# One encoder layer on one core: one of four weight sums per seven-product group on another engine

## The chip, the cores and the metric

The kernel runs on one core of one Trainium2 chip. The metric is the device time of one execution in microseconds, as the median of several runs.

## The reference

One layer of an encoder trunk is computed in float32 on 512 tokens of width 2048. What matters here is the second half of the layer, the feed-forward part; the first half (two kinds of sequence mixing, of which only the time is of interest) comes before it.

```python
y = jnp.concatenate([y_attn, y_lru], axis=-1) @ w_out[l]
h = layer_norm(DEEPNORM_ALPHA * h + y, ln1_g[l], ln1_b[l])
f = jnp.square(jax.nn.relu(h @ w_up[l])) @ w_down[l]     # 2048 -> 8192 -> 2048
h = layer_norm(DEEPNORM_ALPHA * h + f, ln2_g[l], ln2_b[l])
```

## The kernel before

Features lie on the partitions, tokens along the free dimension. Every matrix product with float32 accuracy is made of three products in the faster fp32r type: an operand is split into a high half (a copy to fp32r on ScalarE, ACT) and a low half (operand minus high half, on VectorE, DVE), and TensorE (PE) multiplies high by high, high by low and low by high (`product`, lines 831 to 833: eight blocks of 128 rows, 24 matmuls of 128x256 in all).

Most of the feed-forward part is done in groups of seven block products instead of eight (`winograd`, line 838): 30 groups for `w_up` and 27 for `w_down`, 57 in all. A group loads four weight tiles of 128x1024 (`wload`: a11, a21, a22, a12; the DMAs stand on SyncE's queue, SP). From them four sums are made in place on DVE by the helper `tt` (line 836), in this order in the program: T3's sum a11 - a21 into a11, T1's sum a21 + a22 into a21, T2's sum a22 - a11 into a11, and B22's sum a12 - a11 into a12. The seven products B11, T3, T1, X4, B21, B22 and T2 go through PE in that order. Each one's weight is split by `wsplit` (line 799) right before it: line 153 is the copy on ACT that writes `whi`, line 154 the subtraction on DVE that writes `wlo`. There are three buffers for `whi` and three for `wlo` (two in one pool, one in another), so a split for a product can begin only when the product three places earlier is done with its half. The weight tiles themselves have seven buffers (`wraw`, line 813). T1's sum writes the tile that T3's sum reads.

Results of a group stay in four accumulators in PSUM; DVE adds two partial sums (s1, s7) and the group's results, ACT squares them (in the `w_up` part), and a further operand set is written to DRAM (`up_out`).

The operands of the products (oph, opl) stay in SBUF over many groups and are changed four times: once between the two weight matrices and three times within the second. At these places `u_load` (line 872) loads them and splits them on ACT and DVE, and one or two plain products (`classic`, line 720) run in between.

The order of the instructions on each engine's queue is set when the program is built: a planner takes what is ready in its own account of time, by priority; the splits of weights have a priority 100 places ahead of their line. Engines work through their queues in order and wait for each other by semaphores. GpSimd (POOL) does a few small powers for the norms and, at the very end, three normalising instructions (line 190); in the groups it does nothing.

Of the kernel before, what the change touches and what calls it, by code (L numbers as in the profile page):

```python
# [13 lines left out]
ALU = mybir.AluOpType  # L14
# [34 lines left out]
def body(tc, x, pos, vecs, consts, w_in, w_uq, w_kn, w_v, w_rg, w_out, w_up, w_down, out):  # L49
    nc = tc.nc  # L50
    V, A, T, G = nc.vector, nc.scalar, nc.tensor, nc.gpsimd
# [747 lines left out]
    def wsplit(f, n):  # L799
        woff[0] = (32, 0) if n in ("T3", "T1") else FAR  # L800
        with tc.high_priority(offset=PO2):
            w = wsplit_(f)
        woff[0] = FAR
        return w
# [15 lines left out]
    def wload(src):  # L820
        t = wraw(rawn[0])
        rawn[0] += 1
        nc.sync.dma_start(out=t, in_=src)
        return t

    def product(acc, w, n, first):
        wh, wl = w
        sk = dict(skip_group_check=not first)
        for j in range(8):
            ws = slice(j * P, (j + 1) * P)  # L830
            T.matmul(acc, wh[:, ws], oph[n][:, j], start=first and j == 0, stop=False, **sk)  # L831
            T.matmul(acc, wh[:, ws], opl[n][:, j], start=False, stop=False, **sk)  # L832
            T.matmul(acc, wl[:, ws], oph[n][:, j], start=False, stop=j == 7, **sk)  # L833

    def tt(o, x, y, op):
        V.tensor_tensor(out=o, in0=x, in1=y, op=op)  # L836

    def winograd(slabs, evac, hook=lambda n: None):

        a11 = wload(slabs[0])  # L840
        a21 = wload(slabs[2])
        a22 = wload(slabs[3])
        a12 = wload(slabs[1])
        bank = lambda tag, bufs: ps.tile([P, HS], F32, tag=tag, name="st_" + tag, bufs=bufs)
        half = lambda n: ws_p.tile([P, HS], F32, tag=n, name=n, bufs=2)
        a, b, c, d = bank("mm", 3), bank("sc", 2), bank("tr", 3), bank("mm", 3)
        s1, s7 = half("s1"), half("s7")
        product(a, wsplit(a11, "B11"), "B11", True)
        hook("B11")
        A.activation(s1, a, AF.Copy)  # L850
        tt(a11, a11, a21, ALU.subtract)
        product(b, wsplit(a11, "T3"), "T3", True)
        A.activation(s7, b, AF.Copy)  # L853
        tt(a21, a21, a22, ALU.add)
        product(c, wsplit(a21, "T1"), "T1", True)
        tt(s7, s7, c, ALU.add)
        product(b, wsplit(a22, "X4"), "X4", False)
        hook("X4")
        tt(a11, a22, a11, ALU.subtract)
        product(a, wsplit(a12, "B21"), "B21", False)  # L860
        hook("B21")
        evac("c11", a, None)
        tt(a12, a12, a11, ALU.subtract)
        product(c, wsplit(a12, "B22"), "B22", False)
        hook("B22")
        product(d, wsplit(a11, "T2"), "T2", True)
        tt(s1, s1, d, ALU.add)
        evac("c21", s1, b)
        evac("c12", s1, c)
        evac("c22", s1, s7)  # L870
# [13 lines left out]
    for ch in range(NCL, DFF // 256):  # L884
        o = o_tile()

        def evac(which, x, y):
            t = o[:, 2 * int(which[1]) + int(which[2]) - 3, :]
            if y is not None:
                tt(t, x, y, ALU.add)  # L890
                x = t
            A.activation(t, x, AF.Relu)
            A.activation(t, t, AF.Square)
        winograd([w_up[4 * ch + i] for i in range(4)], evac,
                 *([next_ops(0)] if ch == DFF // 256 - 1 else ()))
        up_out(ch, o)
# [46 lines left out]
    for c in range(NCH):  # L943
        if c == 0:
            r_init(0)
        for i in range(KT // 2):
            sl = [w_down[(c * KT + 2 * i) * 2 + q] for q in range(4)]
            if c == NCH - 1 and i == KT // 2 - 1:
                last_pair(sl)
            elif i < NCL2:  # L950
                def evac(n, acc):
                    tt(r[2 * i + n], r[2 * i + n], acc, ALU.add)
                classic(sl, evac, [lambda n=n: u_load(c, n, n) for n in ("T3", "T1", "T2")] if i == 0 else ())
                if i == NCL2 - 1:
                    u_load(c, "T4", "X4")
            else:
                q = rp[i]

                def evac(which, x, y):
                    t = q[:, 2 * int(which[1]) + int(which[2]) - 3, :]  # L960
                    if which == "c11":
                        tt(t, t, x, ALU.add)
                    elif which == "c22":
                        tt(y, y, x, ALU.add)
                        tt(t, t, y, ALU.add)
                    else:
                        tt(t, t, y, ALU.add)
                        tt(t, t, x, ALU.add)
                def prev_stats(n, i=i):
                    if n == "X4" and i == KT // 2 - 2:  # L970
                        u_load(c, "B12", "X4")
                    if n == "B21":
                        for k in (2 * i - 2, 2 * i - 1):
                            to_tokens(r[k], st2, k)
                hook = () if c + 1 < NCH and i < KT // 2 - 1 else \
                    (next_ops(c + 1),) if c + 1 < NCH else (prev_stats,)
                winograd(sl, evac, *hook)
# [69 lines left out]
```

## Time and profile before

| | us |
|---|---|
| median of 3 runs (lowest to highest) | 1984.33 (1983.44 to 1989.12) |
| the profiled execution: its own time | 1982.85 |
| its span, first to last instruction | 1981.1 |
| PE busy in the span | 1931.8 (98%) |
| DVE busy | 1500.4 (76%) |
| ACT busy | 1013.2 (51%) |
| POOL busy | 18.4 (1%) |

The busy time of an engine is the time in which at least one of its instructions runs; matmuls overlap each other, so PE's busy time says that it was fed, not how well. The mean granted clock of TensorE was 0.998 of full speed. The groups of seven products lie between about 740 and 1940 us of the span.

### The profile page before, as it was taken

The numbers are of one execution on the slowest core, as the hardware profiler recorded it, in microseconds if no ns is written. First come the engines' busy times: TensorE is split into PE (matmuls) and PEld (weight loads), VectorE is DVE, ScalarE is ACT, GpSimd is POOL, SyncE is SP. The second block draws the span as 40 slices with busy tenths as digits, with TensorE's granted clock in tenths as the row PEclk, the third lists the DMA queues.
The fourth block names the chain that finished last, engine by engine and source line by source line (L and its number), as shares of the span: only waits on it lengthen the run. The fifth ranks groups of instructions, "written<-read, shape, count | busy, mean of one in ns | idle before, by whom it ended". The sixth has DMA issues, their size and how long they took to land.

```text
span 1981.1 us, 39297 instructions
## 1 busy us (share of the span) xinstructions
PE 1931.8 (98%) x16472; PEld 1899.5 (96%) x16472; DVE 1500.4 (76%) x2147; ACT 1013.2 (51%) x1482; POOL 18.4 (1%) x20
## 2 busy tenths in 40 slices
PE   6999999999999999999999999999999999999997
PEld 6999999888999999999999999999999999999997
DVE  7565655677433598888888888888898888889885
ACT  6556556555322455555555555565464455445453
POOL 1000000000000000000000000000000000000001
PEclk9999999999999999999999999999999999999999
DMA  7222222212233345444544445486364355346232
GB/s 258 80 96 91 88 100 85 65 53 71 96 118 111 122 152 192 170 171 156 184 151 171 171 153 186 152 287 225 127 214 165 111 180 196 116 138 246 101 103 86
DMA packets 113889, 284.19 MB, mean 143 GB/s; under 512 B 10160, under 2 KB 56368, under 8 KB 109616
## 3 DMA queue, kind: packets, MB, share of 16 engines
q1 hardware_dynamic: 113712, 281.68, 41.3%
q8 instruction: 129, 2.11, 0.4%
q14 instruction: 48, 0.39, 0.1%
HBM read 234.19 MB, written 46.14 MB: 142 GB/s over the span
## 4 chain that ended last, share of the span: by engine, by line
PE 87%; DVE 4%; ACT 3%; DMA 2%; issue 2%; POOL 1%; POOLq 0%; SPq 0%; ACTq 0%; DVEq 0%
PE st_mm L831 8%; PE st_mm L832 8%; PE st_mm L833 8%; PE mm L135 7%; PE mm L136 7%; PE mm L134 7%; PE st_tr L833 5%; PE st_sc L831 5%; PE st_sc L833 5%; PE st_tr L831 5%; PE st_tr L832 5%; PE st_sc L832 5%; PE mm L718 1%; PE mm L716 1%; PE mm L717 1%
## 5 line engine op out<-in xcount | busy, mean ns | idle before, releaser
L153 ACT ACTIVATE whi<-raw 128x1024 fp32r<-128x1024 f32 x399 | 423.5, 1063 | 513.2 <-DVE raw L836 251.9
L154 DVE TENSOR_TENSOR wlo<-raw,whi 128x1024 fp32r<-128x1024 f32 x399 | 484.4, 1221 | 128.8 <-ACT whi L153 121.4
L836 DVE TENSOR_TENSOR raw<-raw 128x1024 f32<-128x1024 f32 x228 | 278.2, 1220 | 3.6
L122 DVE TENSOR_TENSOR wlo<-raw,whi 128x1024 fp32r<-128x1024 f32 (+1 forms) x128 | 141.2, 1104 | 166.8 <-PE mm L136 112.1
L121 ACT ACTIVATE whi<-raw 128x1024 fp32r<-128x1024 f32 (+1 forms) x128 | 123.1, 967 | 203.3 <-PE mm L135 159.8
L134 PE MATMUL mm<-hh,whi 128*128 128x256 f32 x704 | 195.4, 278 | 2.7 <-ACT xp L403 1.9
L136 PE MATMUL mm<-hh,wlo 128*128 128x256 f32 x704 | 195.5, 278 | 0.8 <-DVE wlo L122 0.8
L135 PE MATMUL mm<-hl,whi 128*128 128x256 f32 x704 | 196.0, 278 | 0.0
L134 PEld LDWEIGHTS mm<-hh,whi 128*128 128x128 f32 x704 | 132.8, 189 | 3.1 <-ACT xp L403 2.1
L136 PEld LDWEIGHTS mm<-hh,wlo 128*128 128x128 f32 x704 | 132.9, 189 | 1.0 <-DVE wlo L122 1.0
L135 PEld LDWEIGHTS mm<-hl,whi 128*128 128x128 f32 x704 | 132.9, 189 | 0.0
L831 PE MATMUL st_sc<-X4h,whi 128*128 128x256 f32 x456 | 126.6, 278 | 2.2 <-ACT s L853 2.2
L831 PE MATMUL st_tr<-B22h,whi 128*128 128x256 f32 x456 | 126.6, 278 | 1.9 <-ACT whi L153 1.9
L833 PE MATMUL st_sc<-T3h,wlo 128*128 128x256 f32 x456 | 126.5, 277 | 1.0 <-DVE wlo L154 1.0
L831 PE MATMUL st_mm<-B21h,whi 128*128 128x256 f32 x456 | 126.0, 276 | 0.5 <-ACT s L850 0.5
L831 PE MATMUL st_mm<-T2h,whi 128*128 128x256 f32 x456 | 126.0, 276 | 0.4 <-ACT whi L153 0.4
L833 PE MATMUL st_tr<-B22h,wlo 128*128 128x256 f32 x456 | 126.1, 277 | 0.2 <-DVE wlo L154 0.2
L832 PE MATMUL st_sc<-X4l,whi 128*128 128x256 f32 x456 | 126.3, 277 | 0.0
L831 PE MATMUL st_sc<-T3h,whi 128*128 128x256 f32 x456 | 126.1, 277 | 0.0
L833 PE MATMUL st_sc<-X4h,wlo 128*128 128x256 f32 x456 | 126.1, 277 | 0.0
L832 PE MATMUL st_sc<-T3l,whi 128*128 128x256 f32 x456 | 126.1, 277 | 0.0
L833 PE MATMUL st_mm<-B11h,wlo 128*128 128x256 f32 x456 | 126.0, 276 | 0.0
(440 smaller groups left out, 6464.5 us busy)
## 6 DMA issues: line engine op xcount, KB each, us to landing
raw<-in_w_up SPq DMA_DIRECT2D x128, 512.0 KB, 3.4
raw<-in_w_down SPq DMA_DIRECT2D x128, 512.0 KB, 3.5
u_dram<-uo SPq DMA_DIRECT2D x32, 1024.0 KB, 3.8
raw<-in_w_in SPq DMA_DIRECT2D x50, 512.0 KB, 3.2
raw<-in_w_out SPq DMA_DIRECT2D x32, 512.0 KB, 3.2
X4l<-u_dram SPq DMA_DIRECT2D x18, 512.0 KB, 5.3
x<-in_x SPq DMA_DIRECT2D x8, 512.0 KB, 7.0
h_dram<-hf SPq DMA_DIRECT2D x32, 128.0 KB, 2.5
```

Of the source, the lines that this page charges most:

```text
L121: A.activation(hi[:, :w], raw[:, :w], AF.Copy)
L122: V.tensor_tensor(out=lo[:, :w], in0=raw[:, :w], in1=hi[:, :w].bitcast(F32), op=ALU.subtract)
L134: T.matmul(acc[:, c], wh, xh[:, c], start=first and t == 0, stop=False)
L135: T.matmul(acc[:, c], wh, xl[:, c], start=False, stop=False)
L136: T.matmul(acc[:, c], wl, xh[:, c], start=False, stop=last and t == 1)
L153: A.activation(hi, f, AF.Copy)
L154: V.tensor_tensor(out=lo, in0=f, in1=hi.bitcast(F32), op=ALU.subtract)
L716: T.matmul(o, wh[:, ws], oph[b][:, j], start=first and t == 0, stop=False)
L831: T.matmul(acc, wh[:, ws], oph[n][:, j], start=first and j == 0, stop=False, **sk)
L832: T.matmul(acc, wh[:, ws], opl[n][:, j], start=False, stop=False, **sk)
L833: T.matmul(acc, wl[:, ws], oph[n][:, j], start=False, stop=j == 7, **sk)
L836: V.tensor_tensor(out=o, in0=x, in1=y, op=op)
```

## The change

T1's sum goes from DVE to GpSimd: same operands, same place in the program. The two other lines shown are unchanged and stand for the place.

```diff
         tt(a11, a11, a21, ALU.subtract)
         product(b, wsplit(a11, "T3"), "T3", True)
         A.activation(s7, b, AF.Copy)
-        tt(a21, a21, a22, ALU.add)
+        G.tensor_tensor(out=a21, in0=a21, in1=a22, op=ALU.add)
         product(c, wsplit(a21, "T1"), "T1", True)
         tt(s7, s7, c, ALU.add)
```

## Rows read from the trace of the kernel before

**Rows 1.** Stretches: length, busy PE, PEld, DVE, ACT, POOL (instructions); clock, DMA, GB/s.
```profile
1200.00:1219.08 19.08, 19.08 (x171) 19.08 (x170) 16.00 (x20) 10.41 (x17) 0.00 (x0) 1.00 0.46 165
...
1633.68:1652.76 19.08, 18.77 (x165) 18.57 (x164) 19.08 (x22) 10.70 (x11) 0.00 (x0) 1.00 0.93 316
```
**Rows 2.** Waits of PE, 740 to 1940 us: total us, times, longest.
```profile
PE st_sc L831 <- ACT s L853: 2.2, 3, 1.3
...
PE st_sc L833 <- DVE wlo L154: 1.0, 2, 0.5
...
PE st_tr L833 <- DVE wlo L154: 0.2, 1, 0.2
```
**Rows 3.** Instructions of line 836: count, shortest/median/longest ns, first and last start.
```profile
L836 DVE TENSOR_TENSOR raw<-raw x228: 1204/1219/1226, 742.7 to 1923.8; 128x1024 f32<-128x1024 f32 x114
```
**Rows 4.** DVE in order of time, one group: start us, us, instruction, count, idle before.
```profile
1199.73 2.48 DVE L836 TENSOR_TENSOR raw<-raw 128x1024 f32<-128x1024 f32 x2
1202.14 1.23 DVE L154 TENSOR_TENSOR wlo<-raw,whi 128x1024 fp32r<-128x1024 f32 x1
...
1203.62 1.22 DVE L836 TENSOR_TENSOR raw<-raw 128x1024 f32<-128x1024 f32 x1
1204.75 1.22 DVE L154 TENSOR_TENSOR wlo<-raw,whi 128x1024 fp32r<-128x1024 f32 x1
...
1206.88 1.22 DVE L154 TENSOR_TENSOR wlo<-raw,whi 128x1024 fp32r<-128x1024 f32 x1
...
1213.62 2.38 DVE L154 TENSOR_TENSOR wlo<-raw,whi 128x1024 fp32r<-128x1024 f32 x2 [0.85 <-ACT whi L153]
1217.55 1.23 DVE L154 TENSOR_TENSOR wlo<-raw,whi 128x1024 fp32r<-128x1024 f32 x1 [1.54 <-ACT whi L153]
```
**Rows 5.** ACT in order of time, the same group.
```profile
1201.05 1.06 ACT L153 ACTIVATE whi<-raw 128x1024 fp32r<-128x1024 f32 x1 [1.89 <-DVE raw L836]
1202.76 1.07 ACT L153 ACTIVATE whi<-raw 128x1024 fp32r<-128x1024 f32 x1 [0.65 <-PE st_mm L832]
1205.48 1.06 ACT L153 ACTIVATE whi<-raw 128x1024 fp32r<-128x1024 f32 x1 [1.65 <-PE st_mm L832]
```
**Rows 6.** Groups by line from 1960 us (busy, mean ns), and DVE's line 190.
```profile
L190 POOL TENSOR_SCALAR R<-R,mvh,rsh 128x512 f32<-128x512 f32 x3 | 6.7, 2253 | 0.1
L190 DVE TENSOR_SCALAR R<-R,mvh,rsh 128x512 f32<-128x512 f32 x4 | 2.3, 611 | 0.0
L190 DVE TENSOR_SCALAR R<-R,mvh,rsh x25: 535/540/832, 680.1 to 1974.2; 128x512 f32<-128x512 f32 x25
```
**Rows 7.** PE in order of time, where T3 and T1 begin, the same group.
```profile
1205.63 0.28 PE L833 MATMUL st_sc<-T3h,wlo 128*128 128x256 f32 x1
1208.13 0.28 PE L831 MATMUL st_tr<-T1h,whi 128*128 128x256 f32 x1
1208.36 0.28 PE L833 MATMUL st_tr<-T1h,wlo 128*128 128x256 f32 x1
```
**Rows 8.** DVE's sums and PE's T3 products behind two operand changes, by time.
```profile
1651.97 2.48 DVE L836 TENSOR_TENSOR raw<-raw 128x1024 f32<-128x1024 f32 x2
1660.27 0.28 PE L831 MATMUL st_sc<-T3h,whi 128*128 128x256 f32 x1
1809.69 1.22 DVE L836 TENSOR_TENSOR raw<-raw 128x1024 f32<-128x1024 f32 x1
1813.42 1.22 DVE L836 TENSOR_TENSOR raw<-raw 128x1024 f32<-128x1024 f32 x1
1815.97 2.35 DVE L154 TENSOR_TENSOR wlo<-raw,whi 128x1024 fp32r<-128x1024 f32 x2
1816.34 0.28 PE L831 MATMUL st_sc<-T3h,whi 128*128 128x256 f32 x1
```
**Rows 9.** SP's issues in order of time, and DVE's wait for loads, 740 to 1940.
```profile
1206.00 2.46 SPq L823 DMA_DIRECT2D raw<-in_w_up  x2
DVE wlo L154 <- DMA raw<-in_w_up: 3.1, 2, 1.5
```

## The prediction

> **What bounds the kernel now.** I read first the table of stretches. In the part with the seven-product groups (from 740 to 1940 us) one group takes 19.08 us, and PE is busy for 19.08 of them at the full clock (1.00), DVE for 16.00, ACT for 10.41, POOL for nothing [rows 1]. So PE sets the pace there and DVE has 3.08 us of each group left. Then I read the waits of PE over the same 1200 us: seven rows, from 2.2 us down to 0.2 us (2.2 + 1.9 + 1.0 + 0.5 + 0.4 + 0.3 + 0.2), 6.5 us in all, some 0.5% of the stretch [rows 2]. That is the most that any help to DVE or ACT can give back there. Last I read one steady group in order of time on DVE, ACT and PE, to see how long before its use each weight half is ready; this decides whether a slower sum is noticed.
>
> **The change part by part.** It takes from each of 57 groups one sum on DVE and puts it on POOL. The line of the helper has 228 sums of this kind, four to a group, with a median of 1219 ns [rows 3], so DVE loses 57 x 1.22 = 69.5 us of work. PE does not wait for DVE's share of work but for single instructions, so by [rows 2] the removal alone is worth between 0 and 6.5 us; I take 0, since none of these waits stands in the steady groups.
>
> Where the sum stands: at 1199.73 DVE runs two sums, T3's and T1's, 2.48 us together. T3's ends at 1199.73 + 1.22 = 1200.95, T1's at 1202.21 [rows 4]. T1's sum writes a21, which T3's reads, so on POOL it can't begin before 1200.95. The same kind of hand-over from DVE to ACT takes 0.10 us: ACT's copy for T3 starts at 1201.05 [rows 5]. I let POOL start at 1201.05 as well.
>
> What it costs on POOL: the trace has no sum of this size there. The low end is DVE's own 1.22 us. POOL's only large instructions are three with 128x512 elements, two arithmetic steps and one input, 2253 ns each [rows 6]. Scaled by elements to 1024 this gives 4.51 us, the high end; scaled by arithmetic steps (512 x 2 there, 1024 x 1 here) it gives 2.25 us. I take 2.25 us, the value of the nearest row with an equal count of steps, and keep both ends. The Trainium skill's "GPSIMD Engine Reference" (section "Elementwise — side-by-side cycle accounting") gives 4497 ns for this sum with 2048 elements, so an estimate of 2.25 us for 1024 by that page; no run here shows it.
>
> With 2.25 us the sum is ready at 1203.30, 1.09 us later than now. First ACT: its copy for T1 starts at 1202.76, held until then by the weight buffer and not by the sum, and takes 1.07 us [rows 5]. It would start at 1203.40 and end at 1204.47. PE's first T1 product with that half starts at 1208.13 [rows 7]: 3.7 us to spare. ACT's next copy, at 1205.48, waits for PE and is not touched. Then DVE: T1's second half now runs 1204.75 to 1205.97 [rows 4], after ACT's copy in both cases, and PE asks for it at 1208.36 [rows 7]: 2.4 us to spare. Ahead of it DVE's queue has T3's half (1202.14) and T2's sum (1203.62), which don't depend on POOL; behind it stand the group's results and X4's half. So with engines that don't disturb each other nothing is late and DVE is even 1.2 us earlier.
>
> Does POOL hold up DVE? No row has a DVE instruction with two SBUF inputs beside a large one of POOL. The nearest are the four normalising ones of DVE while POOL's three run: 611 ns in the mean against a median of 540 and a longest of 832 [rows 6], so the low end is next to nothing per instruction, and the high end is that DVE stands still while POOL works. The Trainium skill's "SBUF — State Buffer" (section "Who interferes with whom") states the high end as a rule: a DVE instruction with two SBUF inputs and a reading GpSimd instruction exclude each other, and the second waits for the whole of the first. Rows 6 can't confirm it, since those DVE instructions have one input.
>
> At the high end DVE's next two-input instruction, T3's half at 1202.14, starts at 1203.30, 1.16 us late. It ends at 1204.52; PE asks for it at 1205.63 [rows 4, 7], 1.1 us to spare. All that follows on DVE is 1.16 us late too: T1's half ends at 1207.13 against 1208.36 (1.2 us to spare), X4's at 1206.88 + 1.22 + 1.16 = 1209.26 against 1211.09 (one product after T1's use, 1208.36 - 1205.63 = 2.73 us; 1.8 us to spare). The idle gaps of 0.85 and 1.54 us [rows 4] then take up the 1.16 us before the next group. DVE's load would be 16.00 - 1.22 + 2.25 = 17.03 us of 19.08. So in the steady groups the cost is 0 with either end.
>
> The stretches where the operands are changed are tighter: from 1633.68 on DVE is busy for all 19.08 us [rows 1]. But there T3's sum runs at 1651.97 while PE begins T3 only at 1660.27 [rows 8], so 1.1 us is hidden. At the last change T3's sum is at 1809.69 and T1's at 1813.42, before two halves that start at 1815.97 [rows 8]; PE starts T3 at 1816.34, and by the waits it stands 0.5 us for a half in that neighbourhood. There I bound the change by -0.5 (relieved of the sum) and +1.05 (blocked) and take +0.5. With four such changes the bounds are -2 and +4 us.
>
> The DMA queue: a21's buffer comes free with T1's half, at most 1.2 us later. SP issues two loads at 1206.00, just after that half [rows 9]; seven buffers and four loads a group put the next user of the slot 1.75 groups (33 us) on. In the whole first part DVE waits for a weight load for 3.1 us in two cases [rows 9]. No cost.
>
> Sum against the profiled execution of 1982.85 us: 1982.85 + 0 (57 steady places) + 0.5 = 1983.4. The median of the three runs, 1984.33, lies 1.5 us above that execution, so I expect about 1985 in the median.
>
> **The rivals.**
> 1. POOL needs near 4.5 us and DVE is shut out meanwhile (slower). POOL runs 1201.05 to 1205.56; T3's half ends at 1206.78, PE wanted it at 1205.63: 1.15 us late in every group, since each group's chain hangs on PE's own progress and starts with the same lead again. 57 x 1.15 = 66 us, 2049 us. DVE's load of 16.00 - 1.22 + 4.51 = 19.29 us also passes 19.08. It decides from a sum of 3.4 us on (1205.63 - 1.22 - 1201.05 = 3.36). For it: POOL's rows by element. Against it: the count of steps, and that both conditions are needed; with 4.5 us alone T1's copy ends at 1206.7 and its half at 1207.9, still before 1208.36. This is where the rule of the page on SBUF would act; by it and the page on GPSIMD together (2.25 us) the time would stay.
> 2. The order of the queues changes (slower). The queues' order is fixed when the program is built. If T1's copy is put behind X4's because its sum is late, it takes the next free weight buffer, the one whose copy now starts at 1205.48 [rows 5], and ends at 1206.54; its half then ends at 1207.9 at the earliest, 0.5 us ahead of PE. One more two-input instruction of 1.22 us ahead of it makes it 0.7 us late: 57 x 0.7 = 40 us, 2023 us; a part of the groups or a part of the 0.7 us gives less. Against it: the slack is used up only if several things coincide.
> 3. DVE's relief ends PE's waits (faster). At most 6.5 us, 1978 in the median. Against it: these waits hang on single instructions, mostly ACT's, at the changes of operands.
>
> **How the numbers follow.** No change: 0.70, with 1982 to 1989 as its own range; rival 1: 0.15; rival 2: 0.10; rival 3: 0.05, half of it beyond 0.3%. What a measurement of this kernel can tell from no change is about 0.3%, 6 us. Rival 1 lies wholly beyond that, and so does nearly all of rival 2: slower 0.25, faster 0.03, same 0.72. The range is 1979 to 2010: the likeliest case, nearly all of rival 3, and the lower half of rival 2; rival 1 and the upper half of rival 2 (0.20) are left out.
>
> **What would show each step.** POOL has 57 new sums of some 2.25 us, each starting about 0.1 us after T3's sum; above 3.4 us the forecast is in danger. DVE's busy time in a steady group falls to about 14.8 us, and T3's half starts at its old distance from T3's sum (1.2 us to the end of the sum) or when POOL ends, which tells whether POOL shuts DVE out. PE stays busy for 19.08 of 19.08 us. The prediction is wrong if PE gets a wait for T3's or T1's half, or for ACT's copy for T1, that comes back in each group.

## The result and the profile after

| | before | changed |
|---|---|---|
| median, us (lowest to highest, 4 runs each) | 1985.58 (1983.44 to 1989.12) | 2002.87 (1999.89 to 2004.45) |
| the profiled execution, us | 1982.85 | 1999.89 |
| span, us | 1981.1 | 1998.1 |

The ratio is 1.0087 (95% interval 1.0074 to 1.0100): slower by some 17 us. This lies inside the stated range of 1979 to 2010, but not in its likeliest case: the forecast was no change, 1985 us.

Busy time first. The lines are from the page's group table of the changed kernel (busy us, mean ns of one; then idle time before them):

```profile
L154 DVE TENSOR_TENSOR wlo<-raw,whi 128x1024 fp32r<-128x1024 f32 x399 | 550.3, 1391 | 142.0 <-ACT whi L153 138.2
L854 POOL TENSOR_TENSOR raw<-raw 128x1024 f32<-128x1024 f32 x57 | 137.1, 2405 | 1096.4 <-DVE raw L836 779.1
L836 DVE TENSOR_TENSOR raw<-raw 128x1024 f32<-128x1024 f32 x171 | 209.1, 1223 | 4.2
```

POOL's 57 sums take 2405 ns each. DVE has 57 sums fewer (171 for 228 in [rows 3]), but its weight halves have become longer: 550.3 us where the page of before has 484.4 us for the same 399. The difference, 65.9 us, is 1.16 us for each POOL sum, and it eats the 69.5 us that were taken away. 54 of the 399 halves are lengthened; the longest takes 2518 ns, where it was 1227. DVE's busy time has even risen, from 1500.4 to 1512.6 us.

The waits of PE from 740 to 1960 us (total us, times, longest), which answer to [rows 2]:

```profile
PE st_sc L831 <- ACT s L853: 10.8, 30, 0.5
PE st_mm L831 <- ACT s L850: 1.9, 1, 1.9
PE st_tr L833 <- DVE wlo L154: 1.2, 2, 0.8
PE st_sc L833 <- DVE wlo L154: 1.2, 2, 0.8
PE st_mm L831 <- ACT whi L153: 0.4, 1, 0.4
PE mm L718 <- DVE wlo L122: 0.3, 1, 0.3
```

One row has changed: X4's product waits for line 853, ACT's copy of s7, 30 times, where it was 3 times and 2.2 us. Waits of line 833 for weight halves (`wlo`) are four where they were three. Of the 30 waits for line 853, 28 stand in the first part (`w_up`), one in each group but its first and its last, and two in the second part, each behind a change of operands (at 1483 and 1798 us). The distance from one T1 product on PE to the next says the same (worked out from the start of T1's first matmul in each group):

| | before | changed |
|---|---|---|
| first part, mean of 28 groups, us | 19.08 | 19.70 |
| second part, groups between two operand changes, us | 19.08 | 19.08 |

28 x 0.625 = 17.5 us (the mean is 19.705 before rounding): this is the whole loss. (All else adds up to some -0.2 us up to the last group: 1.1 us less before the first one, 0.9 us more at the operand changes and in the group behind the first of them.)

Now one group of the first part. DVE of the changed kernel in order of time (start us, us, instruction, idle before):

```profile
1035.62 1.23 DVE L836 TENSOR_TENSOR raw<-raw 128x1024 f32<-128x1024 f32 x1
1038.04 2.43 DVE L154 TENSOR_TENSOR wlo<-raw,whi 128x1024 fp32r<-128x1024 f32 x1 [1.19 <-ACT whi L153]
1040.50 1.23 DVE L836 TENSOR_TENSOR raw<-raw 128x1024 f32<-128x1024 f32 x1
1041.64 1.22 DVE L154 TENSOR_TENSOR wlo<-raw,whi 128x1024 fp32r<-128x1024 f32 x1
1042.78 0.41 DVE L836 TENSOR_TENSOR s<-s,st_mm 128x256 f32<-128x256 f32 x1
1043.23 0.42 DVE L836 TENSOR_TENSOR uo<-s,st_sc 128x256 f32<-128x256 f32 x1
```

POOL in the same stretch:

```profile
1036.98 2.40 POOL L854 TENSOR_TENSOR raw<-raw 128x1024 f32<-128x1024 f32 x1 [17.23 <-DVE raw L836]
```

ACT in the same stretch:

```profile
1043.68 0.75 ACT L892 ACTIVATE uo<-uo 128x256 f32<-128x256 f32 x2 [1.23 <-DVE uo L836]
1044.34 0.71 ACT L893 ACTIVATE uo<-uo 128x256 f32<-128x256 f32 x2
1044.95 0.41 ACT L892 ACTIVATE uo<-uo 128x256 f32<-128x256 f32 x1
1045.26 0.37 ACT L850 ACTIVATE s<-st_mm 128x256 f32<-128x256 f32 x1
1045.53 0.41 ACT L893 ACTIVATE uo<-uo 128x256 f32<-128x256 f32 x1
1045.83 1.05 ACT L153 ACTIVATE whi<-raw 128x1024 fp32r<-128x1024 f32 x1
1046.78 0.37 ACT L853 ACTIVATE s<-st_sc 128x256 f32<-128x256 f32 x1
```

And PE, the first matmul of T1 and the place where X4 follows:

```profile
1044.03 0.28 PE L831 MATMUL st_tr<-T1h,whi 128*128 128x256 f32 x1
...
1046.64 0.28 PE L833 MATMUL st_tr<-T1h,wlo 128*128 128x256 f32 x1
1047.20 0.39 PE L831 MATMUL st_sc<-X4h,whi 128*128 128x256 f32 x1 [0.29 <-ACT s L853]
```

T3's half was issued at 1038.04, while POOL's sum ran; it took 2.43 instead of 1.22 us and ended at 1040.47, which is 1.09 us after POOL's end (1039.38). So it did its own work only once POOL was through. From there the delay runs on: DVE's result sums of the group before (`uo`), ACT's squares of them (lines 892, 893), the weight copy for B21, and behind all these in ACT's queue the copy of s7, which empties the accumulator that X4's product goes on adding to. The same chain in the kernel before, ACT in order of time:

```profile
1206.44 0.71 ACT L892 ACTIVATE uo<-uo 128x256 f32<-128x256 f32 x2
...
1209.50 0.37 ACT L853 ACTIVATE s<-st_sc 128x256 f32<-128x256 f32 x1
```

The first result sum on DVE, of before, from which this chain follows:

```profile
1205.89 0.41 DVE L836 TENSOR_TENSOR uo<-s,st_sc 128x256 f32<-128x256 f32 x1
```

and the matmul of PE, of before, that needs the copy:

```profile
1210.86 0.28 PE L831 MATMUL st_sc<-X4h,whi 128*128 128x256 f32 x1
```

Set against the start of T1's product (1208.13 in [rows 7], 1044.03 now):

| us from T1's first matmul | before | changed | later by |
|---|---|---|---|
| T3's half ends (DVE) | -4.76 | -3.56 | 1.20 |
| first result sum starts (DVE) | -2.24 | -0.80 | 1.44 |
| copy of s7 ends (ACT) | 1.74 | 3.12 | 1.38 |
| X4's first matmul (PE) | 2.73 | 3.17 | 0.44 |

The copy had 0.99 us to spare before and is now 1.38 us later. Over the groups from 860 to 1280 us X4 starts 0.51 us later behind T1 in the mean (3.23 for 2.72 us), and its product takes 0.12 us more (the first matmul behind the wait takes 0.39 for 0.28 us): together the 0.62 us, within rounding.

### The profile page after: what moved, and what is told of

It reads as the page before. It is cut to its first block, busy times and chain, and to the rows that moved or that the text cites. A ratio compares the mean times of both kernels' runs of the same rounds, so it can differ in the third digit from the quotient of the medians.

```text
span 1998.1 us, 39464 instructions
## 1 busy us (share of the span) xinstructions
PE 1939.8 (97%) x16472; PEld 1901.1 (95%) x16472; DVE 1512.6 (76%) x2090; ACT 1014.6 (51%) x1482; POOL 155.2 (8%) x77
## 4 chain that ended last, share of the span: by engine, by line
PE 64%; DVE 16%; ACT 11%; issue 6%; DMA 2%; POOL 0%; ACTq 0%; SPq 0%; DVEq 0%; POOLq 0%
DVE wlo L154 8%; PE mm L136 7%; PE mm L134 7%; PE mm L135 7%; ACT whi L153 5%; PE st_mm L831 4%; PE st_mm L832 4%; PE st_mm L833 4%; PE st_sc L831 4%; PE st_sc L833 4%; PE st_sc L832 4%; PE st_tr L833 2%; PE st_tr L831 2%; PE st_tr L832 2%; DVE raw L836 2%
## 5 line engine op out<-in xcount | busy, mean ns | idle before, releaser
L154 DVE TENSOR_TENSOR wlo<-raw,whi 128x1024 fp32r<-128x1024 f32 x399 | 550.3, 1391 | 142.0 <-ACT whi L153 138.2
L854 POOL TENSOR_TENSOR raw<-raw 128x1024 f32<-128x1024 f32 x57 | 137.1, 2405 | 1096.4 <-DVE raw L836 779.1
L836 DVE TENSOR_TENSOR raw<-raw 128x1024 f32<-128x1024 f32 x171 | 209.1, 1223 | 4.2
L833 PE MATMUL st_tr<-T1h,wlo 128*128 128x256 f32 x456 | 126.0, 276 | 0.5 <-DVE wlo L154 0.5
```

Source lines behind the costliest of these rows:

```text
L154: V.tensor_tensor(out=lo, in0=f, in1=hi.bitcast(F32), op=ALU.subtract)
L854: G.tensor_tensor(out=a21, in0=a21, in1=a22, op=ALU.add)
```

## The experiments

The theory, A: POOL's sum and a DVE instruction with two SBUF inputs shut each other out; DVE is therefore late by 1.2 us, and the chain of result sums, squares and copy of s7 has only 1.0 us to spare. Rival R1: the planner's new order on DVE's queue is the cause (the addition into s1 moved behind T2's sum and T1's half; ACT, PE and SP kept their order). Rival R2: the sum itself comes late on POOL, or each hand-over costs.

### s7_early: the copy of s7 one place ahead in ACT's queue

```diff
 # in the changed kernel
-        A.activation(s7, b, AF.Copy)
+        with tc.high_priority(offset=60): A.activation(s7, b, AF.Copy)
```

> The changed kernel, with the copy of s7 (line 853, ACT) one place further ahead in ACT's queue: before the weight copy for B21 (1.06 us) and not behind it. Theory A (POOL holds DVE's next half for some 1.2 us, so DVE's sums of the group before, ACT's squares behind them and at last ACT's copy of s7 come late, and X4's product waits for that copy for 0.5 to 0.6 us in each of 28 groups): the copy ends at 45.9 + 0.37 = 46.2 where PE wants it at 46.75, so the wait is gone, the groups of the first part are 19.08 us again and the time is 1984 to 1988. POOL's instruction still takes 2.4 us and DVE's half for T3 still 2.4 us. Rival R2 (the sum itself is late on POOL and T1's weight halves with it): T1's halves are as late as before, 2000 to 2004.

Measured: 1989.15 us against 1985.13 (ratio 1.0018, 1.0009 to 1.0027), so 13 to 14 of the 17 us are back. ACT's queue in a group now:

```profile
1040.31 0.40 ACT L893 ACTIVATE uo<-uo 128x256 f32<-128x256 f32 x1
1040.62 0.37 ACT L853 ACTIVATE s<-st_sc 128x256 f32<-128x256 f32 x1
1040.88 1.05 ACT L153 ACTIVATE whi<-raw 128x1024 fp32r<-128x1024 f32 x1
```

PE has no wait for line 853 among its longest any more; POOL's sums (2405 ns) and the held half (1051.95, 2.42 us in the next group) are as they were. R2 falls: the sum is just as late, and most of the loss is gone. The groups are not quite at 19.08 but at 19.19 us in the mean. Product by product it is B22 that has become longer there, 2.82 for 2.72 us; its low half now ends only some 0.1 us before the matmul that reads it (1047.16 for 1047.27 in the group shown). The planner had also put one more DVE instruction (line 736) ahead of B21's half. The expectation's 1984 to 1988 was missed by 1 us; what is left in the groups is 28 x 0.11 = 3 us.

### s1_early: the addition into s1 ahead of T1's half again

```diff
 # in the changed kernel
-        tt(s1, s1, d, ALU.add)
+        with tc.high_priority(offset=100): tt(s1, s1, d, ALU.add)
```

> The changed kernel, with the addition into s1 put back ahead of T1's half on DVE's queue (the planner had moved it behind T2's sum and T1's half; now it stands only behind T2's sum). Rival R1 (the loss comes from the new order on DVE's queue): 1985 to 1990, as the result sums no longer follow the addition they need. Theory A: as many instructions stand between T3's half and the group's results as before, so only the 0.12 us by which the result sum started late after the addition is saved, 28 x 0.1 = 3 us: 1996 to 2003.

Measured: 2000.18 us against 1985.13 (1.0069, 1.0055 to 1.0083); a group of the first part takes 19.57 us. The wait row stays:

```profile
PE st_sc L831 <- ACT s L853: 7.9, 31, 0.9
```

So the addition's place ahead of T1's half is worth 0.13 us of the 0.62, as theory A had it. It still stands behind T2's sum, which it did not before, so this run alone undoes half of the new order. R1 as the cause falls with idle_sum_1024 below, where DVE's queue has its old order throughout and a group loses more.

### b22_pool: B22's sum on POOL instead of T1's

```diff
 # in the kernel before
-        tt(a12, a12, a11, ALU.subtract)
+        G.tensor_tensor(out=a12, in0=a12, in1=a11, op=ALU.subtract)
```

> Another of the four sums on POOL: B22's (a12 - a11), T1's back on DVE. POOL then works about 1211.0 to 1213.4 in the time of the steady group of before, where DVE has additions from PSUM and a gap of 0.85 us and where no result of the group before is behind it. Theory A: nothing that ACT's queue needs for s7 is held up; B22's copy ends at 1214.6 and its half at 1215.8 against 1216.5 on PE: 1983 to 1989. A theory by which any sum on POOL costs its hand-over (0.6 us a group): 2000 to 2004.

Measured: 1989.95 us against 1985.13 (1.0017, 1.0009 to 1.0026), 1 us above the expected range. The groups of the first part are at 19.08 us again, so a sum on POOL costs nothing where no late chain stands behind it. The rest lies elsewhere: in its profile 4.3 us are lost before the first group, where nothing was changed, and some 4 us around the operand changes, where ACT and DVE have got their operand splits and weight splits in another order. Why the 4.3 us are lost stays open, and that the new order costs the other 4 us is not shown.

### second_part_only: T1's sum on POOL in the second part alone

```diff
 # in the changed kernel; ws_up[0] is True in the first part, False in the second
-        G.tensor_tensor(out=a21, in0=a21, in1=a22, op=ALU.add)
+        (V if ws_up[0] else G).tensor_tensor(out=a21, in0=a21, in1=a22, op=ALU.add)
```

> T1's sum on POOL only in the 27 groups of the second weight matrix, on DVE in the 30 groups of the first. Theory A: the second part has no squares in ACT's queue, its steady groups stay at 19.08 us, so the time is that of before within 3 us: 1983 to 1989. A theory by which the cost is spread over all 57 groups (0.3 us each): 27 x 0.3 = 8 us more, 1991 to 1995.

Measured: 1985.18 us against 1985.13 (1.0001, 0.9989 to 1.0013). A steady group of the second part (length; busy PE, PEld, DVE, ACT, POOL; clock, DMA share, GB/s):

```profile
1404.72:1423.80 19.08, 19.08 (x170) 19.08 (x169) 16.43 (x20) 7.98 (x9) 2.41 (x1) 1.00 0.34 111
```

POOL's sum is there, DVE is held there as well (16.43 for 16.11 us before), and PE loses nothing. In this part ACT has no squares ahead of the copy of s7.

### idle_sum_1024 and idle_sum_512: a sum that nobody reads

The kernel before, with the queues of PE, DVE and ACT in their old order and a spare sum on POOL in the 30 groups of the first part. `scr` holds a spare tile in the first part and is empty in the second; the lines that make it are left out here. With 512 columns all three operands are cut to `[:, :512]`.

```diff
         tt(a21, a21, a22, ALU.add)
+        if scr: G.tensor_tensor(out=scr[0], in0=a21, in1=a22, op=ALU.add)
```

> The kernel before with nothing moved, and in each of the 30 groups of the first part one more sum on POOL, a21 + a22 into a spare tile that nobody reads, behind T1's sum; the order on every other queue is that of before. It costs only what POOL's reading does to others. Theory A (a POOL sum of 2.4 us and a DVE instruction with two SBUF inputs exclude each other): T3's half or T2's sum on DVE stands until POOL ends, some 2.0 to 2.4 us late; the copy of s7 has 1.0 us to spare, so X4's product is 1.0 to 1.4 us late in each group: 2010 to 2030. Rival R2 (what cost time was that the sum T1 needs was late): nothing is late, 1983 to 1989.

> The same with half the columns in the spare sum (512, some 1.2 us on POOL). Theory A: DVE is held for 0.9 to 1.2 us, about as much as the copy of s7 has to spare (1.0 us), so 0 to 0.3 us a group: 1984 to 1995, and clearly less than half of what the sum with 1024 columns costs. A cost per POOL instruction or per hand-over would be the same as with 1024 columns.

Measured: 2011.59 us against 1984.46 (1.0141, 1.0124 to 1.0158) with 1024 columns, 1984.34 us (0.9999, 0.9989 to 1.0008) with 512. With 1024 columns, POOL and then DVE:

```profile
1064.90 3.29 POOL L854 TENSOR_TENSOR scr<-raw 128x1024 f32<-128x1024 f32 x1 [16.77 <-DVE raw L836]
```

```profile
1064.69 1.23 DVE L154 TENSOR_TENSOR wlo<-raw,whi 128x1024 fp32r<-128x1024 f32 x1
1065.84 0.41 DVE L836 TENSOR_TENSOR s<-s,st_mm 128x256 f32<-128x256 f32 x1
1066.17 3.10 DVE L836 TENSOR_TENSOR raw<-raw 128x1024 f32<-128x1024 f32 x1
```

With 512 columns, POOL and then DVE:

```profile
1050.04 2.19 POOL L854 TENSOR_TENSOR scr<-raw 128x512 f32<-128x512 f32 x1 [16.89 <-DVE raw L836]
```

```profile
1051.31 2.00 DVE L836 TENSOR_TENSOR raw<-raw 128x1024 f32<-128x1024 f32 x1
```

Here DVE was first: with 1024 columns T3's half (1064.69) keeps its 1.23 us, and POOL's sum shows 3.29 for 2.40 us, so it is POOL that waited. Then POOL has its turn, and T2's sum is held until 1.08 us after POOL's end (1069.27 against 1068.19). The addition into s1, with one input from PSUM, runs through in 0.41 us meanwhile. T2's sum is late by 1.88 us with 1024 columns and by 0.78 us with 512. The spare time was 0.99 us, so the first costs 1.01 us a group (20.09 us) and the second nothing (19.08 us). No result depends on these sums; what costs is the holding alone, and only beyond the spare time.

### idle_fill, late_fill, late_sum: does a POOL that only writes hold DVE?

```diff
 # idle_fill, at the place of the spare sum
+        if scr: G.memset(scr[0], 0.0)
 # late_fill and late_sum, behind T1's product in the kernel before
         product(c, wsplit(a21, "T1"), "T1", True)
+        if first_part: G.memset(a21, 0.0)
+        if first_part: G.tensor_tensor(out=a21, in0=a21, in1=a22, op=ALU.add)
```

(late_fill has the first of the two last lines, late_sum the second.)

> The same with a fill of the spare tile (1024 columns, POOL writes and reads nothing) in place of the spare sum. Theory A in the form that reading is what excludes: no DVE instruction is lengthened, 1983 to 1989. If any POOL instruction held DVE, DVE's halves would be lengthened by the fill's own time.

Measured: 1988.42 us against 1984.46 (1.0021, 1.0011 to 1.0030), but not where it was meant to be. The fills depend on nothing, so POOL ran all 30 before the groups, and the groups stayed at 19.08 us. There, in the norm, some 3.9 us were lost (720.89 for 716.98 in the lines below). DVE of this kernel in that stretch:

```profile
700.51 3.41 DVE L190 TENSOR_SCALAR R<-R,mvh,rsh 128x512 f32<-128x512 f32 x3
...
720.89 5.76 DVE L792 TENSOR_TENSOR R<-R 128x1024 f32<-128x1024 f32 x5
```

DVE of the kernel before, the same instructions:

```profile
700.49 1.45 DVE L190 TENSOR_SCALAR R<-R,mvh,rsh 128x512 f32<-128x512 f32 x3
...
716.98 5.76 DVE L792 TENSOR_TENSOR R<-R 128x1024 f32<-128x1024 f32 x5
```

The fills run without a pause from 700.35 to 727.90. They did not lengthen the sums with two inputs (5.76 us in both), but did lengthen scaling instructions that read one SBUF tile (3.41 for 1.45 us): five of the seven beside the fills take 1.07 to 1.27 us, the two others 0.58 and 0.53. Why those two got by stays open.

> The kernel before with, in each of the 30 groups of the first part, a fill of a21 on POOL (1024 columns, 1.0 us, it writes and reads nothing) as soon as T1's halves are made; the order on every other queue is that of before. It stands there beside DVE's result sums and X4's half. Theory A in the form that two reading instructions exclude each other: no two-input instruction of DVE is lengthened in the groups (none over 1.3 us), 1983 to 1989. If any POOL instruction held them, the third result sum and with it ACT's copy of s7 would be some 0.4 us late, still within its 1.0 us: the durations tell the two apart and not the time.

Measured: 1984.08 us against 1984.04 (0.9994, 0.9983 to 1.0006). POOL and DVE of this kernel in one group:

```profile
959.62 0.96 POOL L855 MEMSET raw<- 128x1024 f32 x1 [18.17 <-issue]
```

```profile
960.09 0.42 DVE L836 TENSOR_TENSOR uo<-s,s 128x256 f32<-128x256 f32 x1
```

Line 836 of this kernel, the third result sum, in all 30 groups (count, shortest/median/longest ns):

```profile
L836 DVE TENSOR_TENSOR uo<-s,s x30: 419/422/425, 769.3 to 1329.2; 128x256 f32<-128x256 f32 x30
```

> The same place with a sum in place of the fill (a21 + a22 into a21 once T1's halves are made, 1024 columns, 2.4 us; nobody reads it). Theory A: it starts about 1206.0 in the time of the steady group of before, DVE's third result sum (two inputs from SBUF) at 1206.55 stands until 1208.4 and is 1.9 us late, X4's half behind it too; ACT's square of the third result and the copy of s7 behind it come some 1.6 us late against 1.0 us to spare, so 0.6 to 1.2 us a group: 2000 to 2022. A theory by which only what depends on the sum is late: 1983 to 1989.

Measured: 1994.32 us against 1984.04 (1.0056, 1.0039 to 1.0073), with the same row:

```profile
L836 DVE TENSOR_TENSOR uo<-s,s x30: 426/2244/2257, 768.1 to 1338.0; 128x256 f32<-128x256 f32 x30
```

At one and the same place a fill leaves the result sum at 422 ns and a sum makes it 2244 ns. The time of late_sum was expected too high (2000 to 2022): a group loses 0.35 us and not 0.6 to 1.2. The first two results, with one input from PSUM, are not held (0.42 us) and ACT squares them meanwhile, so the copy of s7 ends some 1.2 us late behind T1's first matmul and not 1.6 (2.97 us in the group at 1022 us, 1.74 before).

## Why the prediction was right or wrong, point by point

- **What bounds the kernel: right.** PE was fed in every steady group of the kernel before, and the second part, where it still is, kept its time.
- **POOL's price: nearly right.** 2.25 us was taken, 2.405 us measured; the row scaled by arithmetic steps was the right neighbour, the one scaled by elements (4.51) not.
- **POOL shuts DVE out: the high end is true.** The prediction kept both ends (next to nothing; DVE stands still while POOL works). T3's half was expected 1.16 us late at that end and was 1.20 us late. The Trainium skill's "SBUF — State Buffer" (section "Who interferes with whom") states this exclusion. The traces agree with it: two-input DVE instructions wait for POOL's end with its 2405 ns sum, POOL waits where DVE came first (3.29 for 2.40 us), the addition with one input from SBUF and one from PSUM runs through (0.41 us), and a fill leaves two-input sums alone (422 ns).
- **"So in the steady groups the cost is 0 with either end": wrong, and this is the step that failed.** "All that follows on DVE is 1.16 us late too" was right, but what follows was checked for the weight halves of T1 and X4 alone (1.2 and 1.8 us to spare). Those did hold. The result sums stood in the same queue, named in the prediction as "behind it", and were not followed to ACT. There the copy of s7 stands behind their squares and a weight copy, in order, with 0.99 us to spare: 1209.87 for a matmul at 1210.86. This was to be read in the trace of before; s7_early (the wait goes) and idle_sum_512 against idle_sum_1024 (0.78 us late is free, 1.88 us costs 1.01 us) show that this spare time decides. The prediction's own signs of being wrong were waits for T3's or T1's half or for ACT's copy for T1; none of them came back in each group, and the wait that did (for the copy of s7) stood in no sign.
- **Rivals.** Rival 1 asked for a sum above 3.4 us, and its place (T3's half on PE) was not where the time went. Rival 2 (queue order, ACT's copy for T1 behind X4's) did not happen: ACT's and PE's orders are the same as before; DVE's order did change, but the part of it that s1_early undid is worth 0.13 of 0.62 us a group. That the time lies in the range is luck: the range reached so far up for the lower half of rival 2, whose mechanism was not there. Rival 3 found nothing to gain.
- **Operand changes and DMA: right in size.** The changes cost 0.9 us in all (0.5 taken, bounds -2 to +4), and no wait for a weight load stands among PE's.
- **DVE's busy time: wrong.** In a steady group it was to fall from 16.0 to 14.8 us. It is 16.2 us in a group of the first part (16.23 from 1200.00 to 1219.70), as the held instruction counts as busy; 17.03 us was worked out for the high end.

## What to carry to other kernels

When an instruction is made late by a known amount, follow every consumer behind it in its queue, on the other engines and in their queues as well, down to the next instruction of the engine that sets the pace, and take the smallest spare time found, not that of the data in the change. Work given to an engine that takes turns with the relieved one may free nothing: here 69.5 us left DVE and 65.9 us came back as waiting. The same move is free where no such chain stands behind the held instruction (the second part: 1985.18 for 1985.13 us), so what stands behind it decides, and not its duration alone.

## What the runs showed of the hardware

- A POOL sum of two SBUF inputs and a DVE instruction of two SBUF inputs take turns, whole instructions at a time: a held DVE instruction of 128x1024 ends 1.08 to 1.09 us after POOL's end in three kernels, one of 128x256 0.28 us after it (late_sum: POOL until 1022.56, DVE until 1022.84), and its waiting is recorded as its own duration, on POOL as on DVE (2.43 for 1.22, 3.29 for 2.40 us).
- A fill on POOL (0.96 to 1.00 us for 128x1024) leaves two-input instructions alone but held five of seven scaling instructions of DVE from SBUF to SBUF (3.41 for 1.45 us for the first three).
- A wait costs PE more than the waits' row shows: the 28 waits of the first part are 9.8 us in the row and 17.5 us in the groups. Matmuls in a stream start every 0.11 us and are recorded as 0.28 us long, so 0.16 us of overlap is lost before the row starts to count, and the matmul behind the wait is recorded 0.11 us longer, with the next one 0.23 us behind it (1047.20 and 1047.43).
